# GpSimd shares the low parts of the weights beside the choice of keys, with two pauses and a root moved

## The chip, the cores and the metric

The kernel runs on one core of a Trainium2 chip. The metric is the device time of one execution in microseconds (us). The engines are named as in the profile: PE (matrix products), PEld (its weight loads), DVE (VectorE), ACT (ScalarE), POOL (GpSimd) and SP (SyncE).

## The reference

All in float32, for 512 tokens of width 1024: two hybrid layers (dilated attention, mLSTM, MLP), then one layer with three mixers, which is the one that the change touches:

```python
def _layer(h, ...):
    xn = _rmsnorm(h, norm1_w)
    proj = xn @ w_in
    z, xbc, dt_raw, q, k, v, qi, ki, wi, u, gates = _split_proj(proj)
    xbc = jax.nn.silu(_causal_dwconv(xbc, conv_w, conv_b))
    xs, Bm, Cm = jnp.split(xbc, ...)
    dt = jax.nn.softplus(dt_raw + dt_bias)
    y = _ssd_scan(xh, dt, -jnp.exp(a_log), Bm, Cm)
    y = y + d_skip * xh
    y_ssd = _rmsnorm(y * jax.nn.silu(z), ssd_norm_w)
    y_att = _dsa_attention(qh, kh, vh, qi, ki, wi)
    y_pool = _pool_mixer(u, pool_w, pool_scale)
    g = jax.nn.sigmoid(gates)
    merged = g0 * (y_ssd @ w_up_ssd) + g1 * (y_att @ w_up_attn) + g2 * (y_pool @ w_up_pool)
    h = h + merged @ w_out
    hn = _rmsnorm(h, norm2_w)
    a_part, b_part = jnp.split(hn @ w_ffn_in, 2, axis=-1)
    return h + (jax.nn.silu(a_part) * b_part) @ w_ffn_out

def _dsa_attention(q, k, v, qi, ki, wi):      # for each block of 128 queries
    s = einsum(qi, ki)                        # 4 index heads
    score = einsum(relu(s), wi)               # masked to earlier keys
    idx = top_k(score, 128)                   # the choice of keys
    ...                                       # softmax attention over the chosen keys
```

## The kernel before

**Products.** Each float32 product is three: with a weight split into a high part `wh` and a low part `wl`, and an input into `h` and `l`, `lin` (L281 to L283) adds h·wh, l·wh and h·wl in one PSUM bank `pb`. Weights come as chunks of 128x1024, two tiles of columns each, in the order of their use. `chunk` (L217 to L253) makes one: a DMA on SP's queue brings `wr`, ACT copies it to `wh` (L248), and DVE subtracts the two for `wl` (L249). `wr`, `wh` and `wl` have three buffers each. Where a call has a lead of 2, the two chunks of a pair are worked side by side: here called the first (A) and the second (B) chunk.

**Background work.** The smaller parts are Python generators that `start` registers with a rate. After each group of three products `tick` adds the rate to a counter and takes one step of the generator for each whole number reached; a bare `yield` ends a step, `pause(k)` yields PAUSE[k] times, and `join` runs out what is left. So rates and yields set where the small instructions stand among the large products on each engine, and each engine runs its own instructions in that order. All their PSUM tiles (`br`, `tp`, `bt`, `bb`, `bp`, `yo`, `is`, `bc`, `cs`) share two banks.

**The stage in question.** Behind the convolution the program starts `ssd` in the background of the projections z, qi, k, v and q. The SSD first makes decays: `br` (L1384) is copied to `bs` by ACT, what is left of it is `slo` on DVE (L1389), written into `bs` (L1390). Then, for each of two groups, four transposes to `tp` (L1399), copied as `bt`; sixteen more transposes `tp` (L1408), each four of which DVE scales to `xd` (L1410); states; and a tail of decays: DVE's `le` (L1465), ACT's exponential, POOL's `le` (L1467), PE's `bp` (L1473), `yo` (L1478) and `yd` (L1485), then `cvo` on DVE (L1493), POOL (L1494) and DVE (L1495). After `join(ssd)` the SSD's sum of squares goes through `colsum` (four transposes `cs`, L349, and a reduction, L351), `rsqrt` (twelve small DVE instructions, L365 to L371) and `rowbc` (`hc`, `lc`, two products `dg` on DVE, L339, and two matmuls `bc`, L340). The same root for the layer's input (`rabc`) stands just ahead of `join(ssd)`; it serves eight scalings of `x` on DVE (L1191).

Then `idx`, the indexer, is started beside the gates and the SSD's projection (`branch`), later beside u and the pool mixer. It splits `ki`, makes the scores `is` of each block of queries (L437, L438), rectifies them on ACT (`ir`, L1341), adds them on DVE (L1342), and chooses the keys by 16 rounds of MAX8 and MATCH_REPLACE8 on DVE (L1347, L1348), for three blocks of 256, 384 and 512 keys.

Of the kernel before, what the change touches and what calls it, by code (L numbers as in the profile page):

```python
# [10 lines left out]
F32 = mybir.dt.float32  # L11
# [3 lines left out]
ALU = mybir.AluOpType  # L15
# [4 lines left out]
D = 1024  # L20
NB = 4
# [20 lines left out]
def cols(a, n=P):  # L42
    return np.arange(a, a + n)
# [84 lines left out]

RATE = {"att1": 0.437, "rec": 0.556, "ssd": 0.5, "idx": 0.45, "att2": 0.704, "pool": 0.219}

AHEAD = 2

PAUSE = {"cs": 2, "lf": 5, "cols": 2, "fr": 10, "sum": 1}

LEAD = {"conv": 0, "mo": 0, "ga": 0, "gb": 2, "pa": 2, "pb": 0, "z": 0, "qi": 2, "kv": 2, "q": 2, "br": 2, "up": 2, "u": 2}

# [12 lines left out]
class Build:  # L151
    def __init__(self, nc, tc, ctx, dram, at, recipes):
        self.nc, self.tc = nc, tc
        self.dram, self.at = dram, at
        self.recipes = recipes
        self.nchunk = 0
        pool = lambda **k: ctx.enter_context(tc.tile_pool(**k))
        self.cp = pool(name="cp", bufs=1)
        self.tp = pool(name="tp", bufs=59)
        self.sp = pool(name="sp", bufs=3)  # L160
        self.wp = pool(name="wp", bufs=3)
        self.pm = pool(name="pm", bufs=4, space=PSUM)
        self.pw = pool(name="pw", bufs=2, space=PSUM)
        self.uid = 0
        self.bg = []


    def name(self, s):
# [44 lines left out]
    def pause(self, k):  # L213
        for _ in range(PAUSE[k]):
            yield


    def chunk(self, key, l, rows, cs, keep=False):

        nc = self.nc  # L220
        kt, m = len(rows) // P, len(cs)
        i = self.nchunk
        self.nchunk += 1
        self.recipes.append((key, l, rows, cs))
        n = kt * m
        if i < 2:
            raw = self.raw[i]
        else:
            raw = self.wp.tile([P, CHUNK], F32, name=self.name("wr"), tag="wr")
            nc.sync.dma_start(raw[:, :n], self.dram["w"][i, :, :n])  # L230
        src = raw[:, :n]
        if keep:
            out = [], []
            for k in range(0, kt, 4):
                c = src[:, k * m : min(k + 4, kt) * m]
                for o, part in zip(out, self.split(c, n=c.shape[-1])):
                    o.extend(part[:, x * m : x * m + m] for x in range(min(4, kt - k)))
            return out
        h = self.wp.tile([P, CHUNK], F32R, name=self.name("wh"), tag="wh")
        lo = self.wp.tile([P, CHUNK], F32R, name=self.name("wl"), tag="wl")  # L240
        if i < 2:
            for a, b in FIRST:
                with self.behind(a // P - 1):
                    nc.scalar.activation(h[:, a:b], src[:, a:b], AF.Copy)
                    nc.vector.tensor_tensor(lo[:, a:b], src[:, a:b], h[:, a:b].bitcast(F32), ALU.subtract)
            return tuple(x[:, :n].rearrange("p (k m) -> p k m", k=kt) for x in (h, lo))
        with self.behind(KD - 1 if i == 2 else -1):
            nc.scalar.activation(h[:, :n], src, AF.Copy)  # L248
            nc.vector.tensor_tensor(lo[:, :n], src, h[:, :n].bitcast(F32), ALU.subtract)  # L249
        v = lambda x: x[:, :n].rearrange("p (k m) -> p k m", k=kt)  # L250
        return v(h), v(lo)

# [371 lines left out]
    def hybrid(self, l, xs, acc):  # L624
# [44 lines left out]
        def tok(col, brow, out):  # L669
            bb = self.t("bb")  # L670
            nc.gpsimd.dma_start(bb, self.dram[brow][l : l + 1, :].partition_broadcast(P))

            def ev(b, ps):
                o = self.t("tok")
                v.scalar_tensor_tensor(o, ps, rcol[:, b : b + 1], bb, ALU.mult, ALU.add)
                out.append(o)

            self.lin_tok("w_in", l, cols(col, T), xs, ev)

        def prep(i, x):  # L680
# [352 lines left out]
    def second(self, xs, st):  # L1033
        nc = self.nc
# [5 lines left out]
        rbc, first = None, {}  # L1040
# [11 lines left out]
        def store(dst):  # L1052
            def ev(j, ps):
                o = self.t("p")
                v.tensor_tensor(o, ps, rbc, ALU.mult)
                dst[j] = o

            return ev
# [34 lines left out]
        stz = {"acc": None}  # L1093
        ssd = self.start(self.ssd(xc, dtw3, zs, ys, stz), RATE["ssd"])

# [8 lines left out]
        self.lin_cols("w_in_2", 0, [cols(Z2 + j * P) for j in range(8)], xs, ev_z, lead=LEAD["z"])  # L1104
        qi = [None] * 2
        self.lin_cols("w_in_2", 0, [cols(QI2 + j * P) for j in range(2)], xs, store(qi), lead=LEAD["qi"])
        kv = [None] * 2
        self.lin_cols("w_in_2", 0, [cols(K2), cols(V2)], xs, store(kv), lead=LEAD["kv"])
        vtok = self.t("vtok")
# [9 lines left out]
            q[j] = o  # L1119

        self.lin_cols("w_in_2", 0, [Q2 + QPERM[j * P : j * P + P] for j in range(4)], xs, ev_q, lead=LEAD["q"])
        rabc = self.rowbc(self.rsqrt(first["sum"], NB, 1.0 / D, "rn"))
        self.join(ssd)
        ssum = self.colsum([stz["acc"]])
        sr = self.rsqrt(ssum, NB, 1.0 / D, "rs")
        srb = self.rowbc(sr)
        bias = [None] * NB
        idx = self.start(self.indexer(qi, ki, wi, bias), RATE["idx"])


        m = [None] * 8
# [32 lines left out]
        pool = [None]  # L1164

        def pooled(j):
            if j == 4:
                u = [None] * 4
                self.lin_cols("w_in_2", 0, [cols(U2 + i * P) for i in range(4)], xs, store(u), lead=LEAD["u"])
                pool[0] = self.start(self.pool(u, yp), RATE["pool"])  # L1170

        branch(0, 0, "w_up_ssd_2", ys, extra=srb, hook=pooled)
        self.join(pool[0])

        self.join(idx)
        ya = []
        kk = [self.stack_k(kv[0], x) for x in range(2)]
        att = self.start(
# [6 lines left out]
            ),  # L1185
            RATE["att2"],
        )
# [72 lines left out]
        for tk, c in zip(parts, acc):  # L1260
            n = tk.stop - tk.start
            for j in range(TAIL, 8):
                sq = add(j, tk)
            cs = self.ps("cs")[:, :n]
# [54 lines left out]
    def indexer(self, qi, ki, wi, bias):  # L1319
        nc = self.nc  # L1320
        v = nc.vector
        bias[0] = self.t("b0")
        v.tensor_scalar(bias[0][:, 0:P], self.c("maskI"), NEG, None, ALU.max)
        qA = []
        for h in range(4):
            qA.append(self.stack_q(qi[h // 2], h % 2))
            yield
        B, C = self.split(ki)
        yield
        for I in range(1, NB):  # L1330
            n = P * (I + 1)
            sc = self.t("sc")
            for h in range(4):
                sp = self.ps("is")
                self.dots(sp, qA[h], B, C, I * P, n)
                wcol = wi[:, 4 * I + h : 4 * I + h + 1]
                if h == 0:
                    v.tensor_scalar(sc[:, :n], sp[:, :n], 0.0, wcol, ALU.max, ALU.mult)
                else:
                    r = self.t("ir")  # L1340
                    nc.scalar.activation(r[:, :n], sp[:, :n], AF.Relu)  # L1341
                    v.scalar_tensor_tensor(sc[:, :n], r[:, :n], wcol, sc[:, :n], ALU.mult, ALU.add)  # L1342
                yield
            v.tensor_tensor(sc[:, I * P : n], sc[:, I * P : n], self.c("maskI"), ALU.add)
            for _r in range(16):
                m8 = self.s("m8", 8)
                v.max(m8, sc[:, :n])  # L1347
                v.match_replace(sc[:, :n], m8, sc[:, :n], TAKEN)  # L1348
                yield
            v.tensor_scalar(sc[:, :n], sc[:, :n], TAKEN, NEG, ALU.not_equal, ALU.mult)  # L1350
            bias[I] = sc

    def ssd(self, xc, dtw3, zs, ys, stz):
        nc = self.nc
# [15 lines left out]
        cs = self.ps("cs")  # L1370
        nc.tensor.matmul(cs[:, 0:64], tri, a, start=True, stop=True)
        nc.tensor.matmul(cs[:, 64:128], self.ones, a, start=True, stop=True)
        bt = self.s("sbt", 128, bufs=1)
# [14 lines left out]
        lo = self.t("slo")[:16]  # L1388
        v.tensor_tensor(lo, br[0:16, :], bs[0:16, :].bitcast(F32), ALU.subtract)  # L1389
        v.tensor_copy(bs[32:48, :], lo)  # L1390
        yield
        for gi in range(2):
            sel = self.t("selp", F32R)
            src = self.c("sel")[:, 8 * gi : 8 * gi + 8].unsqueeze(2).to_broadcast([P, 8, 64])
# [4 lines left out]
                nc.tensor.transpose(tp[:, c * P : c * P + P], xc[8 + gi][:, c * P : c * P + P], idn)  # L1399
            btok = self.t("bt")  # L1400
            nc.scalar.copy(btok, tp)
            yield
            xd = [None] * NB
            prev = [None] * NB
            for c in range(NB):
# [188 lines left out]
```

## Time and profile before

| | us |
|---|---|
| median of 3 runs | 2461.04 (2460.28 to 2463.59) |
| the profiled execution, its time | 2463.07 |
| its span | 2461.3 |
| PE busy in it | 2432.2 (99%) |
| DVE, ACT, POOL busy | 1450.0 (59%), 1021.0 (41%), 357.2 (15%) |
| mean granted clock of PE | 0.997 of full speed |

The span runs from the first to the last instruction; the execution's time is 1.8 us longer. A busy PE is not PE at its peak: consecutive products overlap, so a product's length is longer than the distance of two starts, and what counts is the idle time in front of an instruction, with the instruction that ended it. In the timelines, a row is the start, the length, engine, line, operation, output and inputs, shape, count, and in brackets the idle time before it and its releaser.

### The profile page before, as it was taken

What the parts mean: (1) busy time and instruction counts of PE and PEld (TensorE: products, weight loads), DVE (VectorE), ACT (ScalarE), POOL (GpSimd) and SP (SyncE); (2) the same over time, 40 slices, a digit from 0 to 9 for tenths busy, and PEclk for the clock granted to TensorE, in tenths of its full rate; (3) what the DMA queues carried; (4) which work ended last, traced back from release to release, by engine and by line L of the source; (5) the groups of instructions that cost most, each with busy time, mean ns of one, the idle gap of its engine ahead of it and who ended that gap; (6) DMA issues with size and microseconds to landing.
All of it is one profiled execution on the core that took longest, in us unless ns stands there. A gap on an engine that the chain in (4) does not pass through costs nothing.

```text
span 2461.3 us, 28093 instructions
## 1 busy us (share of the span) xinstructions
PE 2432.2 (99%) x10858; PEld 1935.1 (79%) x10858; DVE 1450.0 (59%) x2445; ACT 1021.0 (41%) x1514; POOL 357.2 (15%) x301
## 2 busy tenths in 40 slices
PE   9999999999999999999999999999999999999998
PEld 7877788888887877778888888777777788888887
DVE  6686655433446687655433446867898755434345
ACT  4577534332234387633332324444325533322223
POOL 3410010000311520001000030143222100101010
PEclk9999999999999999999999999999999999999999
DMA  4221223333333322223233233221222222333332
GB/s 160 90 82 52 78 80 97 99 94 94 94 94 94 95 78 69 61 86 101 88 96 95 86 106 95 84 82 52 81 87 70 76 80 92 103 95 92 96 91 72
DMA packets 62821, 216.46 MB, mean 88 GB/s; under 512 B 7136, under 2 KB 10464, under 8 KB 62688
## 3 DMA queue, kind: packets, MB, share of 16 engines
q1 hardware_dynamic: 59840, 210.57, 28.0%
q0 software_dynamic: 800, 2.62, 0.3%
q8 instruction: 85, 1.39, 0.2%
q10 hardware_dynamic: 2048, 1.48, 0.2%
q14 instruction: 48, 0.39, 0.0%
HBM read 212.55 MB, written 2.10 MB: 87 GB/s over the span
## 4 chain that ended last, share of the span: by engine, by line
PE 86%; DVE 8%; ACT 2%; issue 2%; DMA 1%; POOL 0%; SPq 0%; DVEq 0%; ACTq 0%; POOLq 0%
PE pb L281 25%; PE pb L282 25%; PE pb L283 25%; DVE wl L249 2%; PE yp L484 1%; PE pb L320 1%; PE pb L321 1%; PE pb L322 1%; PE PT L465 1%; DVE sc L1348 1%; DVE cv L528 1%; DVE m L1347 1%; PE S L964 1%; PE num L971 1%; DVE A L420 1%
## 5 line engine op out<-in xcount | busy, mean ns | idle before, releaser
L281 PE MATMUL pb<-h,wh 128*128 128x512 f32 x2976 | 1197.5, 402 | 2.8 <-DVE qk L646 2.3
L283 PE MATMUL pb<-h,wl 128*128 128x512 f32 x2976 | 1179.7, 397 | 2.9 <-DVE wl L249 2.9
L282 PE MATMUL pb<-l,wh 128*128 128x512 f32 x2976 | 1179.3, 396 | 0.1
L248 ACT ACTIVATE wh<-wr 128x1024 fp32r<-128x1024 f32 (+1 forms) x393 | 410.8, 1055 | 957.3 <-PE pb L282 681.4
L249 DVE TENSOR_TENSOR wl<-wr,wh 128x1024 fp32r<-128x1024 f32 (+1 forms) x393 | 507.0, 1294 | 285.9 <-ACT wh L248 283.0
L281 PEld LDWEIGHTS pb<-h,wh 128*128 128x128 f32 x2976 | 561.0, 189 | 137.2 <-issue 5.1
L283 PEld LDWEIGHTS pb<-h,wl 128*128 128x128 f32 x2976 | 560.6, 188 | 136.3 <-DVE wl L249 4.8
L282 PEld LDWEIGHTS pb<-l,wh 128*128 128x128 f32 x2976 | 561.3, 189 | 132.8 <-issue 5.2
L823 POOL TENSOR_TENSOR y<-y,rbc 128x512 f32<-128x512 f32 x16 | 24.6, 1540 | 573.0 <-DVE y L821 573.0
L1209 DVE TENSOR_TENSOR f<-pb,rbc 128x512 f32<-128x512 f32 x44 | 30.4, 692 | 124.9 <-PE pb L283 124.9
L266 ACT ACTIVATE h<-f 128x512 fp32r<-128x512 f32 x86 | 54.4, 633 | 109.3 <-DVE f L809 88.2
L1213 POOL TENSOR_TENSOR f<-f,fs 128x512 f32<-128x512 f32 x22 | 38.3, 1740 | 406.6 <-ACT fs L1212 406.6
L831 DVE TENSOR_TENSOR x<-x,pb 128x512 f32<-128x512 f32 x40 | 27.5, 688 | 100.4 <-PE pb L283 100.3
L267 DVE TENSOR_TENSOR l<-f,h 128x512 fp32r<-128x512 f32 x86 | 59.4, 691 | 44.4 <-ACT h L266 44.4
L821 DVE TENSOR_TENSOR y<-y,pb 128x512 f32<-128x512 f32 x32 | 22.0, 689 | 92.5 <-PE pb L283 92.5
L528 DVE SCALAR_TENSOR_TENSOR cv<-cz,par,cv 128x512 f32<-128x512 f32 x84 | 67.6, 805 | 12.4 <-ACT cv L526 11.5
L454 ACT ACTIVATE s<-s,ng 128x128 f32<-128x128 f32 (+3 forms) x96 | 53.5, 558 | 33.8 <-DVE ng L453 33.5
L320 PE MATMUL pb<-wh,h 128*128 128x512 f32 x128 | 51.0, 400 | 0.4 <-DVE gt L724 0.4
L737 DVE TENSOR_TENSOR gate<-pb,rbc 128x512 f32<-128x512 f32 x40 | 27.3, 687 | 40.0 <-PE pb L283 39.9
L321 PE MATMUL pb<-wh,l 128*128 128x512 f32 x128 | 50.8, 397 | 0.0
L322 PE MATMUL pb<-wl,h 128*128 128x512 f32 x128 | 50.5, 396 | 0.0
L788 POOL TENSOR_TENSOR m<-m,m 128x512 f32<-128x512 f32 x16 | 26.0, 1623 | 155.0 <-DVE m L787 155.0
(391 smaller groups left out, 2298.6 us busy)
## 6 DMA issues: line engine op xcount, KB each, us to landing
wr<-in_w_dram SPq DMA_DIRECT2D x381, 512.0 KB, 3.6
wr<-in_w_dram SPq DMA_DIRECT2D x16, 448.0 KB, 3.4
x<-in_x_dram POOLq DMA_DIRECT2D x6, 256.0 KB, 5.8
out_dram<-o SPq DMA_DIRECT2D x4, 256.0 KB, 2.4
out_dram<-o ACTq DMA_DIRECT2D x4, 256.0 KB, 2.7
x<-in_x_dram SPq DMA_DIRECT2D x2, 256.0 KB, 4.3
wr<-in_w_dram SPq DMA_DIRECT2D x4, 128.0 KB, 5.7
wr<-in_w_dram SPq DMA_DIRECT2D x2, 256.0 KB, 7.7
```

The costliest lines, as they stand in the source:

```text
L248: nc.scalar.activation(h[:, :n], src, AF.Copy)
L249: nc.vector.tensor_tensor(lo[:, :n], src, h[:, :n].bitcast(F32), ALU.subtract)
L266: nc.scalar.activation(h[:, :n], src, AF.Copy)
L267: nc.vector.tensor_tensor(lo[:, :n], src, h[:, :n].bitcast(F32), ALU.subtract)
L281: mm(ps[:m, :], a, xh, start=k == 0, stop=False)
L282: mm(ps[:m, :], a, xl, start=False, stop=False)
L283: mm(ps[:m, :], b, xh, start=False, stop=k == n - 1)
L320: mm(ps[b], ah, wh[:, kk, :], start=k == 0, stop=False)
L321: mm(ps[b], al, wh[:, kk, :], start=False, stop=False)
L322: mm(ps[b], ah, wl[:, kk, :], start=False, stop=k == 7)
L454: nc.scalar.activation(s[:, :n], s[:, :n], AF.Exp, bias=ng, scale=-1.0, accum_out=ls)
L528: nc.vector.scalar_tensor_tensor(a, z[:, 1 + j : 1 + j + T], w[:, j : j + 1], a, ALU.mult, ALU.add)
```

## The change

Four edits, all in the third layer:

- While the indexer runs (`shared`, from its start to its join) every chunk with an odd number has its subtraction on GpSimd.
- The SSD pauses two steps where it yielded once: behind `bs`, and behind `bt`. The indexer pauses three steps where it yielded once, behind the split of `ki`.
- The root `rabc` is made behind the projection qi, two projections earlier.
- The rates of `ssd` and `idx` are 0.51 and 0.46, from 0.5 and 0.45.

```diff
-RATE = {..., "ssd": 0.5, "idx": 0.45, ...}
+RATE = {..., "ssd": 0.51, "idx": 0.46, ...}
-PAUSE = {"cs": 2, "lf": 5, "cols": 2, "fr": 10, "sum": 1}
+PAUSE = {"cs": 2, "lf": 5, "cols": 2, "fr": 10, "sum": 1, "bt": 2, "is": 3}
...
+        self.shared = False
...
             nc.scalar.activation(h[:, :n], src, AF.Copy)
-            nc.vector.tensor_tensor(lo[:, :n], src, h[:, :n].bitcast(F32), ALU.subtract)
+            sub = nc.gpsimd if self.shared and i % 2 else nc.vector
+            sub.tensor_tensor(lo[:, :n], src, h[:, :n].bitcast(F32), ALU.subtract)
...
         self.lin_cols("w_in_2", 0, [cols(QI2 + j * P) for j in range(2)], xs, store(qi), lead=LEAD["qi"])
+        rabc = self.rowbc(self.rsqrt(first["sum"], NB, 1.0 / D, "rn"))
...
         self.lin_cols("w_in_2", 0, [Q2 + QPERM[j * P : j * P + P] for j in range(4)], xs, ev_q, lead=LEAD["q"])
-        rabc = self.rowbc(self.rsqrt(first["sum"], NB, 1.0 / D, "rn"))
         self.join(ssd)
...
         idx = self.start(self.indexer(qi, ki, wi, bias), RATE["idx"])
+        self.shared = True
...
         self.join(idx)
+        self.shared = False
...
         B, C = self.split(ki)
-        yield
+        yield from self.pause("is")
...
         v.tensor_copy(bs[32:48, :], lo)
-        yield
+        yield from self.pause("bt")
...
             nc.scalar.copy(btok, tp)
-            yield
+            yield from self.pause("bt")
```

The lines behind these stand three to five lower in the changed kernel (L249 is L252 there, L1408 is L1413, L1467 is L1472). PE's work and SP's queue of weight DMAs are the same; ten subtractions go from DVE to POOL, all of them of first chunks of a pair. Rows below are an engine's instructions in its order, each with line, operation, output and inputs.

**The SSD's first transposes, on PE.** Before, from two products ahead of L1399 to the first L1408:

```order
L283 MATMUL pb_12395<-h_11390,wl_12392 128x512
L1399 MATMUL tp_12404<-first,cvo_11794 128x128 x4
L281 MATMUL pb_12395<-h_11434,wh_12391 128x512
L282 MATMUL pb_12395<-l_11435,wh_12391 128x512
L283 MATMUL pb_12395<-h_11434,wl_12392 128x512
L281 MATMUL pb_12395<-h_11478,wh_12391 128x512
L282 MATMUL pb_12395<-l_11479,wh_12391 128x512
L283 MATMUL pb_12395<-h_11478,wl_12392 128x512
L1408 MATMUL tp_12417<-first,cvo_11880 128x128
```

Of the change, the same transposes (L1404 there) and the products behind them; one more product follows these rows, and then the first L1413:

```order
L286 MATMUL pb_12395<-h_11478,wl_12392 128x512
L1404 MATMUL tp_12410<-first,cvo_11794 128x128 x4
L284 MATMUL pb_12395<-h_11522,wh_12391 128x512
L285 MATMUL pb_12395<-l_11523,wh_12391 128x512
L286 MATMUL pb_12395<-h_11522,wl_12392 128x512
L284 MATMUL pb_12395<-h_11566,wh_12391 128x512
L285 MATMUL pb_12395<-l_11567,wh_12391 128x512
L286 MATMUL pb_12395<-h_11566,wl_12392 128x512
L284 MATMUL pb_12395<-h_11610,wh_12391 128x512
L285 MATMUL pb_12395<-l_11611,wh_12391 128x512
L286 MATMUL pb_12395<-h_11610,wl_12392 128x512
L284 MATMUL pb_12395<-h_11654,wh_12391 128x512
```

Twelve products stand between the transposes and the next ones, where six stood; and the first transposes themselves stand six products later.

**The SSD's tail, on POOL.** `le` and `cvo` are the SSD's decays and outputs. Before:

```order
L1467 TENSOR_TENSOR le_13107<-le_13107,cbs_13010 128x512
L1467 TENSOR_TENSOR le_13122<-le_13122,cbs_13010 128x512
L1494 TENSOR_TENSOR cvo_12138<-cvo_12138,eb_13137 128x384
L1467 TENSOR_TENSOR le_13177<-le_13177,cbs_13010 128x512
L1467 TENSOR_TENSOR le_13192<-le_13192,cbs_13010 128x512
L1494 TENSOR_TENSOR cvo_12181<-cvo_12181,eb_13218 128x384
L1467 TENSOR_TENSOR le_13258<-le_13258,cbs_13010 128x512
L1467 TENSOR_TENSOR le_13273<-le_13273,cbs_13010 128x512
L1494 TENSOR_TENSOR cvo_12224<-cvo_12224,eb_13297 128x384
```

Of the change:

```order
L1472 TENSOR_TENSOR le_13162<-le_13162,cbs_13056 128x512
L252 TENSOR_TENSOR wl_13437<-wr_13434,wh_13436 128x1024
L1499 TENSOR_TENSOR cvo_12138<-cvo_12138,eb_13177 128x384
L1472 TENSOR_TENSOR le_13228<-le_13228,cbs_13056 128x512
L1472 TENSOR_TENSOR le_13243<-le_13243,cbs_13056 128x512
L1499 TENSOR_TENSOR cvo_12181<-cvo_12181,eb_13258 128x384
L252 TENSOR_TENSOR wl_13525<-wr_13522,wh_13524 128x1024
L1472 TENSOR_TENSOR le_13307<-le_13307,cbs_13056 128x512
L1472 TENSOR_TENSOR le_13322<-le_13322,cbs_13056 128x512
L1499 TENSOR_TENSOR cvo_12224<-cvo_12224,eb_13337 128x384
L1499 TENSOR_TENSOR cvo_12267<-cvo_12267,eb_13373 128x384
L252 TENSOR_TENSOR wl_13624<-wr_13621,wh_13623 128x1024
```

Three subtractions for weights that are used after the SSD's join stand among its steps, one ahead of the first `cvo`, one ahead of the third pair of `le`, one behind the last `cvo`.

**The root and the indexer's start, on DVE and PE.** On DVE before, from the input's root (dg_13392) into that of the SSD's sum:

```order
L339 TENSOR_TENSOR dg_13392<-first,hc_13387 128x512
L339 TENSOR_TENSOR dg_13395<-first,lc_13388 128x512
L351 TENSOR_REDUCE cs_13404<-cs_13399 128x4
L1191 SCALAR_TENSOR_TENSOR x_99<-x_99,par_9235,rbc_13386 128x512
L365 TENSOR_SCALAR rsx_13406<-cs_13404 128x4
L1191 SCALAR_TENSOR_TENSOR x_100<-x_100,par_9235,rbc_13386 128x512
L366 TENSOR_SCALAR rsa_13408<-rsx_13406 128x4
L1191 SCALAR_TENSOR_TENSOR x_101<-x_101,par_9235,rbc_13386 128x512
L367 TENSOR_SCALAR rsy_13407<-rsa_13408 128x4
L1191 SCALAR_TENSOR_TENSOR x_102<-x_102,par_9235,rbc_13386 128x512
L369 TENSOR_TENSOR rsa_13408<-rsx_13406,rsy_13407 128x4
L249 TENSOR_TENSOR wl_13543<-wr_13540,wh_13542 128x1024
```

Of the change, from the last step of the SSD on:

```order
L385 TENSOR_TENSOR acc_12686<-acc_12686,sq_13396 128x512
L354 TENSOR_REDUCE cs_13404<-cs_13399 128x4
L368 TENSOR_SCALAR rsx_13406<-cs_13404 128x4
L369 TENSOR_SCALAR rsa_13408<-rsx_13406 128x4
L370 TENSOR_SCALAR rsy_13407<-rsa_13408 128x4
L372 TENSOR_TENSOR rsa_13408<-rsx_13406,rsy_13407 128x4
L373 SCALAR_TENSOR_TENSOR rsa_13408<-rsa_13408,rsy_13407 128x4
L252 TENSOR_TENSOR wl_13532<-wr_13529,wh_13531 128x1024
L374 SCALAR_TENSOR_TENSOR rsy_13407<-rsa_13408,rsy_13407 128x4
L372 TENSOR_TENSOR rsa_13408<-rsx_13406,rsy_13407 128x4
```

The scalings of `x` and the first `dg` are gone from the chain (they stand behind rows of the SSD, some 50 rows earlier), and one subtraction of weights stands in it where two stood. On PE 46 products stood between the transposes `cs` of this sum and its first `bc`, and 22 do now. On PE, the indexer's first products before:

```order
L283 MATMUL pb_13539<-h_13362,wl_13536 128x512
L281 MATMUL pb_13546<-h_13362,wh_13542 128x512
L282 MATMUL pb_13546<-l_13363,wh_13542 128x512
L283 MATMUL pb_13546<-h_13362,wl_13543 128x512
L437 MATMUL is_13509<-h_13498,A_13462 128x256
L437 MATMUL is_13519<-h_13498,A_13471 128x256
L438 MATMUL is_13509<-l_13499,A_13462 128x256
L438 MATMUL is_13519<-l_13499,A_13471 128x256
L437 MATMUL is_13553<-h_13498,A_13480 128x256
L438 MATMUL is_13553<-l_13499,A_13480 128x256
```

and of the change:

```order
L285 MATMUL pb_13528<-l_13284,wh_13524 128x512
L440 MATMUL is_13543<-h_13498,A_13462 128x256
L440 MATMUL is_13553<-h_13498,A_13471 128x256
L286 MATMUL pb_13528<-h_13283,wl_13525 128x512
L284 MATMUL pb_13535<-h_13283,wh_13531 128x512
L285 MATMUL pb_13535<-l_13284,wh_13531 128x512
L441 MATMUL is_13543<-l_13499,A_13462 128x256
L441 MATMUL is_13553<-l_13499,A_13471 128x256
L286 MATMUL pb_13535<-h_13283,wl_13532 128x512
L284 MATMUL pb_13528<-h_13362,wh_13524 128x512
```

They stood in a row, 12 products behind the second `bc`; now the first two stand 15 products behind it, and groups of products of weights stand between them.

## Rows read from the trace of the kernel before

**Rows 1.** The page, busy time of each engine over the whole span.

```profile
PE 2432.2 (99%) x10858; PEld 1935.1 (79%) x10858; DVE 1450.0 (59%) x2445; ACT 1021.0 (41%) x1514; POOL 357.2 (15%) x301
```

**Rows 2.** Waits of PE over the whole span: total us, times, longest.

```profile
PE pb L283 <- DVE wl L249: 2.9, 3, 1.3
PE tp L1408 <- DVE slo L1389: 1.6, 1, 1.6
PE bc L340 <- DVE dg L339: 1.1, 4, 0.3
PE is L437 <- ACT h L266: 0.8, 1, 0.8
PE is L437 <- ACT ir L1341: 0.7, 1, 0.7
PE is L438 <- DVE l L267: 0.5, 1, 0.5
```

**Rows 3.** Windows: PE, PEld, DVE, ACT, POOL busy us (instructions); PE clock; DMA; GB/s.

```profile
1740.00:1780.00 40.00, 37.68 (x157) 29.20 (x155) 34.17 (x75) 15.79 (x23) 4.74 (x4) 0.96 0.17 53
1780.00:1820.00 40.00, 38.73 (x169) 31.42 (x169) 39.03 (x91) 7.50 (x9) 8.68 (x8) 1.00 0.37 109
1820.00:1860.00 40.00, 38.36 (x160) 29.55 (x159) 39.45 (x72) 11.86 (x16) 17.50 (x18) 1.00 0.23 72
```

**Rows 4.** Timeline of DVE, two operations ahead of the SSD's transposes.

```profile
1624.43 1.22 DVE L249 TENSOR_TENSOR wl<-wr,wh 128x1024 fp32r<-128x1024 f32 x1 [1.84 <-ACT wh L248]
1625.57 0.67 DVE L1389 TENSOR_TENSOR slo<-br,bs 16x512 f32<-16x512 f32 x1
```

**Rows 5.** Timeline of PE around the indexer's first products.

```profile
1759.76 0.40 PE L282 MATMUL pb<-l,wh 128*128 128x512 f32 x1
1759.99 0.40 PE L283 MATMUL pb<-h,wl 128*128 128x512 f32 x1
...
1761.19 0.50 PE L437 MATMUL is<-h,A 128*128 128x256 f32 x2 [0.80 <-ACT h L266]
...
1765.41 0.63 PE L281 MATMUL pb<-h,wh 128*128 128x512 f32 x1
1765.84 0.63 PE L282 MATMUL pb<-l,wh 128*128 128x512 f32 x1
```

**Rows 6.** Timeline of POOL: its operations beside the SSD and the gates.

```profile
1621.21 1.30 POOL L532 TENSOR_TENSOR cvo<-cv,sg 128x512 f32<-128x512 f32 x1 [3.88 <-ACT sg L530]
...
1711.25 1.28 POOL L1467 TENSOR_TENSOR le<-le,cbs 128x512 f32<-128x512 f32 x1 [1.00 <-ACT le L1466]
1714.04 1.02 POOL L1494 TENSOR_TENSOR cvo<-cvo,eb 128x384 f32<-128x384 f32 x1 [1.51 <-DVE cvo L1493]
...
1723.39 1.92 POOL L1494 TENSOR_TENSOR cvo<-cvo,eb 128x384 f32<-128x384 f32 x1 [0.89 <-DVE cvo L1493]
...
1779.12 4.10 POOL L1141 TENSOR_TENSOR gate<-gate,rbc 128x512 f32<-128x512 f32 x2 [10.28 <-ACT gate L1139]
```

**Rows 7.** Timeline of DVE: operations with two inputs beside those of POOL.

```profile
1621.30 1.29 DVE L1379 TENSOR_TENSOR sdec<-sbt 128x64 f32<-128x64 f32 x1
...
1709.51 1.82 DVE L249 TENSOR_TENSOR wl<-wr,wh 128x1024 fp32r<-128x1024 f32 x1
...
1780.09 1.98 DVE L249 TENSOR_TENSOR wl<-wr,wh 128x1024 fp32r<-128x1024 f32 x1
```

**Rows 8.** Timeline of DVE: the root of the SSD's sum.

```profile
1745.74 0.69 DVE L351 TENSOR_REDUCE cs<-cs 128x4 f32<-128x512 f32 x1 [0.72 <-PE cs L349]
1746.35 0.74 DVE L1191 SCALAR_TENSOR_TENSOR x<-x,par,rbc 128x512 f32<-128x512 f32 x1
1747.01 0.16 DVE L365 TENSOR_SCALAR rsx<-cs 128x4 f32<-128x4 f32 x1
...
1749.28 1.22 DVE L249 TENSOR_TENSOR wl<-wr,wh 128x1024 fp32r<-128x1024 f32 x1
...
1756.04 0.69 DVE L339 TENSOR_TENSOR dg<-first,lc 128x512 fp32r<-128x512 f32 x1
```

More of the change, by code (lines that the diff above doesn't have):

```diff
@@ L127, in params2 @@
     return pack(parts)
-RATE = {"att1": 0.437, "rec": 0.556, "ssd": 0.5, "idx": 0.45, "att2": 0.704, "pool": 0.219}
+RATE = {"att1": 0.437, "rec": 0.556, "ssd": 0.51, "idx": 0.46, "att2": 0.704, "pool": 0.219}
 AHEAD = 2
-PAUSE = {"cs": 2, "lf": 5, "cols": 2, "fr": 10, "sum": 1}
+PAUSE = {"cs": 2, "lf": 5, "cols": 2, "fr": 10, "sum": 1, "bt": 2, "is": 3}
 LEAD = {"conv": 0, "mo": 0, "ga": 0, "gb": 2, "pa": 2, "pb": 0, "z": 0, "qi": 2, "kv": 2, "q": 2, "br": 2, "up": 2, "u": 2}
```

## Prediction

> **What bounds the kernel now.** The page comes first: PE is busy 99% of the span [rows 1], so a change can only win what PE waits or what its clock loses. The list of PE's waits is next [rows 2]. There the reader sees that the waits which the four edits can reach are short: 2.9 us in three waits of weight products for DVE's `wl`, 1.6 us in one of the SSD's transposes `tp` for `slo`, 1.1 us in four waits of `bc`, of which the root that moves has 0.3, and 0.8, 0.7 and 0.5 us of the indexer's products `is`. Then the windows over the choice of keys [rows 3]: DVE is busy 39.03 and 39.45 of 40 us there, more than PE, while POOL works 8.68 and 17.50. In the window ahead of them PE has its one lower granted clock, 0.96.
>
> The timelines give the causes. `slo` is behind a subtraction of weights on DVE [rows 4], and the transposes need the PSUM bank that it frees. The first `is` waits 0.80 us for ACT's split of `ki` and, behind that, two more times; then two starts of weight products are 0.43 us apart, where they were 0.23 us before the waits [rows 5]. That is PE at 1.2 GHz in place of 2.4, after a stretch with gaps. A mean of 0.96 over 40 us is 4% of 40, so 1.6 us were lost by it.
>
> The sum is made against the profiled execution, 2463.07 us. The median of the runs, 2461.04, stands 2.0 lower, and I take 2.0 off at the end. What a measurement can tell from no change is about 0.2%, 4.9 us: faster means under 2456.1, slower over 2466.0.
>
> **What it should win.**
> - *The SSD's transposes.* Six more products stand ahead of `tp` (L1399) and twelve in place of six behind it, so the waiting transposes stand 12 x 0.23 = 2.8 us later against `slo`, which does not move. That is over the wait of 1.6 [rows 2, 4]: gain 1.6, late next nothing that I see (`xd` is made from the same transposes, and the SSD's rate is 2% higher).
> - *The root moved forward.* Its two `dg`, two `bc` and twelve small DVE instructions go among the SSD's second group, where PE has weight products to do; 0.3 us of wait [rows 2] goes. The eight scalings of `x` at 0.74 us [rows 8] go there too, off the chain of the next root; DVE has room there.
> - *The indexer's products.* They start 15 products behind the second `bc`, not 12, which is 0.7 us against the 0.8 waited for `h`; and products of weights now stand between them, so the waits for `l` and `ir` find cover. Of 0.8 + 0.7 + 0.5 = 2.0 us I leave 0.4. If the gaps go, so does the low clock, 1.6 us [rows 2, 3]. Gain 3.2, between 1.0 (waits half left, clock too) and 3.6.
> - *The subtractions on POOL.* Ten at 1.22 us [rows 4] are 12.2 us less on a DVE that is full. The waits for `wl` are of second chunks of a pair, which stay on DVE, so they come forward with DVE. The ten are all first chunks, whose buffers come free a chunk earlier (48 products, 11 us), so POOL has time. I leave 0.5 of 2.9: gain 2.4, between 0 and 2.9.
>
> Sum of gains: 1.6 + 0.3 + 3.2 + 2.4 = 7.5.
>
> **What it should cost.** No row shows a subtraction of 128x1024 on POOL. The nearest are 1.28 us for 128x512 and 1.02 for 128x384 [rows 6]: 0.26 for 128 columns, so 1.28 + 4 x 0.26 = 2.3; twice 1.28 is 2.6. I take 2.4. The upper end is the 128x384 that took 1.92 [rows 6], 1.9 times as long: 4.5.
> - *The SSD's tail.* One subtraction stands ahead of the first `cvo` of POOL, one ahead of a pair of `le`. Behind the late `cvo` DVE waits with the next `le` queued behind it, and PE with `bp` and `yd` behind that. Each can cost PE between 0 (POOL and PE had the slack) and 2.4. From the lengths of the rows I work out some 1.7 for the first and 1.3 for the second, since POOL was idle 1.5 us ahead of its `cvo` and 1.0 ahead of `le` [rows 6]: 3.0, between 0 and 4.8.
> - *The SSD's root.* From the reduction to the end of the second `dg` the chain took 1745.74 to 1756.73 [rows 8], 11.0 us, with 46 products of cover (10.6 us). Now 22 stand there: 5.1 us. The chain loses the eight scalings (8 x 0.66 start to start) and one subtraction (1.2): 11.0 - 5.3 - 1.2 = 4.5 us are left, and the first `bc` needs only the first `dg`, 0.7 sooner. With the 0.7 us that DVE idled for `cs` it is 4.5 against 5.1, no wait at all, if nothing stands in between. But a POOL subtraction stands right there too, behind the last `cvo`, and that holds DVE up.
>
> What shows that is a pair of rows: `sdec`, 128x64, took 1.29 us on DVE beginning 0.09 us behind a POOL operation of 1.30 us, and both end together [rows 6, 7]. A subtraction took 1.98 beside POOL's 4.10 us of gates, and 1.82 beside `le`, not 1.22 [rows 4, 6, 7]. So a DVE operation with two inputs in SBUF can stand still until POOL's ends: the root's chain can lose up to 2.4 us by it. I take 1.3, between 0 and 3.2, and for the others, that a subtraction on DVE now and then takes the rest of a POOL one, which is in the 0.5 that I left above.
>
> The Trainium skill, "SBUF — State Buffer", section "Who interferes with whom", speaks against this change: a DVE instruction with two SBUF inputs contends with a GpSimd one that reads SBUF, and whoever issues first has the shared ports for the whole instruction. The trace agrees (1.29 for a 128x64 operation). Taken strictly, it would make each of the ten a lock of its full length, which is the last rival below.
>
> The two rates and the order of SP's queue cost nothing: the DMAs and PE's work are the same, a yield more or less only moves rows. A chunk's buffer comes free about 1.2 us later on POOL, covered by the 11 us of the chunk that is being used.
>
> Sum: -7.5 + 3.0 + 1.3 = -3.2; 2463.07 - 3.2 - 2.0 = 2457.9, so **2458 us**.
>
> **The rivals.**
> - *No new wait.* The SSD's tail has slack and the root's chain misses POOL's operation. For it: POOL idles 35 of 40 us in the window of the root [rows 3], and 3.88 us ahead of a step of the SSD [rows 6]. Against it: PE's SSD steps follow closely upon each other. -7.5, or -8.4 with nothing left of the waits: 2453.6 to 2452.7.
> - *All is given back.* The tail costs 4.8 and the root 3.2, at their upper ends: +0.5, 2461.5; with the `wl` waits unchanged, 2463.9. For it: the same two rows that show DVE stopped. If the root's `bc` waits that long, the clock may fall as it did at `is`.
> - *The pauses don't do it.* The order moves as said, but the split of `ki` is later too and `is` and `tp` wait as before: gains 0.3 + 2.4 against 4.3, 2462.6. Little speaks for it; it would be a DVE full of what moved.
> - *Slower: DVE is locked by POOL beside the choice of keys.* Each subtraction moved saves DVE 1.2 us. If it stops DVE for more than 1.2 on the mean, DVE has more to do than before, and there it has 0.5 to 1 us left in 40 [rows 3], so PE pays. At the upper length, 4.5, and an arrival in the middle, it stops 2.25, net 1.05 for seven subtractions: +7.4, with 4.3 of other costs and 5.1 of gains: +6.6, 2467.6. For it: the 4.10 us of two gates that should take 2.6 [rows 6]. Against it: POOL already worked 8.68 us beside a full DVE in the window of 1780 to 1820, and PE was busy 38.73 of 40 all the same [rows 3].
>
> **How the numbers follow.** The sum as forecast 0.42, with its own range 2455 to 2461; no new wait 0.27; all given back 0.17; the pauses in vain 0.04; slower 0.10. A third of the forecast, 0.14, lies under 2456.1. Faster: 0.27 + 0.14 = 0.41. Same: 0.28 + 0.17 + 0.04 = 0.49. Slower: 0.10. The range, 2452 to 2464, reaches over the first two rivals and leaves out the slow case and a little at the low end.
>
> **What would show it.** Right: no wait of `tp` for `slo`; PE's clock 1.00 in the window of the indexer's start; under 1 us waited for `wl`; POOL's subtraction near 2.4 us; new waits of `bp` or `yd` near 1.7 and 1.3 us in the SSD's tail, and of `bc` for `dg` near 1.3. Wrong in the good direction: none of the new waits. Wrong in the bad one: a clock under 1.00 behind `bc`, POOL's subtraction over 4 us, and `wl` on DVE at over 2.4 us beside the choice of keys, with waits for `wl` over 3 us.

## The result and the profile after

The changed kernel takes 2477.55 us (median of 6 runs, 2476.49 to 2478.83) against 2460.93 for the kernel before: a ratio of 1.0067 with a 95% interval of 1.0057 to 1.0077, so 16.6 us slower. 2458 was forecast, with a range up to 2464. The profiled execution took 2477.80, its span is 2476.0.

The page of the changed kernel, engines' busy time:

```profile
PE 2436.7 (98%) x10858; PEld 1940.2 (78%) x10858; DVE 1456.2 (59%) x2435; ACT 1020.7 (41%) x1514; POOL 378.6 (15%) x311
```

DVE has ten instructions fewer than before [rows 1] and is busy 6.2 us longer, not 12.2 shorter (5.4 of this comes without the sharing, as experiment 1 shows). PE's list of waits, total, times and longest:

```profile
PE pb L286 <- DVE wl L252: 8.1, 5, 4.3
PE bc L343 <- DVE dg L342: 3.4, 5, 2.2
PE is L440 <- DVE sc L1343: 2.6, 1, 2.6
PE bp L1478 <- DVE le L1470: 2.3, 3, 1.8
```

The waits of `tp` and most of those of `is` for `h`, `l` and `ir` [rows 2] are gone, as forecast. In their place stand 8.1 us for `wl` in place of 2.9, 3.4 for `bc` in place of 1.1, 2.6 of `is` for the bank that `sc` holds on DVE, and 2.3 of `bp`. No wait of PE is for a `wl` that POOL made. The windows, with the columns of [rows 3]:

```profile
1740.00:1780.00 40.00, 35.14 (x159) 26.70 (x158) 30.84 (x60) 13.67 (x21) 11.18 (x8) 0.96 0.21 67
1780.00:1820.00 40.00, 39.85 (x174) 31.98 (x172) 35.57 (x80) 10.56 (x13) 15.77 (x12) 1.00 0.24 79
1820.00:1860.00 40.00, 32.57 (x119) 24.48 (x120) 35.55 (x66) 8.11 (x11) 15.71 (x13) 0.88 0.27 86
```

The window in the middle is better than before (39.85 busy, was 38.73). The last one has only 32.57 of 40 and a granted clock of 0.88; before it had 38.36 and 1.00 [rows 3]. 12% of 40 us is 4.8 us. Some 0.9 of it lies in PE's longest wait itself (from 1850.81 to 1855.51 the granted clock is 0.81), so the clock alone cost some 3.9 us there.

Set beside each other by the position in the sequence of weight products, the two traces are level at 1600 us. The changed kernel is 2.6 us ahead behind the SSD's first transposes, 4.5 behind at the end of the SSD, 6.4 behind at 1780, 5.4 at 1820, 9.3 at 1830 and 15.1 at 1850; from 1900 on the distance stays at 16.1. (Where pauses put a step of the background later, a trace counts as ahead until the step is done.)

Why DVE saved nothing is in its timeline (start, length, operation, idle before):

```profile
1717.71 2.17 DVE L252 TENSOR_TENSOR wl<-wr,wh 128x1024 fp32r<-128x1024 f32 x1
...
1753.90 2.36 DVE L374 SCALAR_TENSOR_TENSOR rsy<-rsa,rsy 128x4 f32<-128x4 f32 x1
...
1770.64 2.30 DVE L1347 SCALAR_TENSOR_TENSOR sc<-ir,wi,sc 128x256 f32<-128x256 f32 x1
...
1773.66 1.21 DVE L252 TENSOR_TENSOR wl<-wr,wh 128x1024 fp32r<-128x1024 f32 x1
...
1820.86 1.84 DVE L1314 TENSOR_TENSOR pt<-pt,p 128x16 f32<-128x16 f32 x1
...
1839.98 2.30 DVE L1347 SCALAR_TENSOR_TENSOR sc<-ir,wi,sc 128x512 f32<-128x512 f32 x1
...
1844.52 1.75 DVE L1312 SCALAR_TENSOR_TENSOR pt<-pt,p 128x496 f32<-128x496 f32 x1 [1.20 <-POOL pt L1306]
...
1850.61 0.68 DVE L1353 MATCH_REPLACE8 sc<-m,sc 128x512 f32<-128x512 f32 x1
...
1854.24 1.22 DVE L252 TENSOR_TENSOR wl<-wr,wh 128x1024 fp32r<-128x1024 f32 x1
```

The row of 1753.90 is an operation on 128x4. One of that size took 0.16 us [rows 8]; this one took 2.36. `sc` (L1347) of 128x256 takes 0.48 undisturbed (so in the kernel before, at 1764.25) and took 2.30 at 1770.64. POOL at those times:

```profile
1718.77 3.38 POOL L252 TENSOR_TENSOR wl<-wr,wh 128x1024 fp32r<-128x1024 f32 x1
...
1753.66 2.57 POOL L252 TENSOR_TENSOR wl<-wr,wh 128x1024 fp32r<-128x1024 f32 x1 [6.18 <-ACT wh L249]
...
1770.26 2.40 POOL L252 TENSOR_TENSOR wl<-wr,wh 128x1024 fp32r<-128x1024 f32 x1 [0.42 <-ACT wh L249]
...
1820.00 2.68 POOL L252 TENSOR_TENSOR wl<-wr,wh 128x1024 fp32r<-128x1024 f32 x1 [3.51 <-ACT wh L249]
...
1839.15 2.58 POOL L252 TENSOR_TENSOR wl<-wr,wh 128x1024 fp32r<-128x1024 f32 x1 [2.30 <-ACT wh L249]
1841.69 1.49 POOL L1306 TENSOR_TENSOR pt<-pt 128x510 f32<-128x510 f32 x1
...
1850.43 2.37 POOL L252 TENSOR_TENSOR wl<-wr,wh 128x1024 fp32r<-128x1024 f32 x1 [2.86 <-ACT wh L249]
```

The long DVE rows of 1753.90, 1770.64, 1820.86 and 1839.98 have two inputs in SBUF. Each begins while a POOL subtraction runs, and ends with it or up to 0.6 us behind it: 1753.90 + 2.36 = 1756.26, POOL 1753.66 + 2.57 = 1756.23; 1770.64 + 2.30 = 1772.94, POOL to 1772.66.

Not every subtraction does this. In the whole trace six of the ten stop one such operation, for some 1.5 to 2.2 us, 10.5 in sum. Two, of 3.38 and 3.50 us, met a subtraction of DVE's and were held up themselves. The other two met only operations that kept their length: the SSD's `le`, which has an input in PSUM, and rounds of the choice of keys (0.68 us for the row of 1850.61, beside POOL's 1850.43, as for its like elsewhere).

The POOL rows of 1839.15 and 1841.69 show a second thing. The pool mixer's `pt` stands behind the subtraction, which itself had to wait for ACT's copy. DVE idles 1.20 us for `pt` and is stopped once more (row 1844.52), here by a product of POOL's gates (1844.44, 1.29 us) and not by a subtraction; the weights' `wl` of 1854.24 is behind that. PE at these places:

```profile
1728.38 0.47 PE L1478 MATMUL bp<-bs,selp 128*128 128x512 f32 x1 [1.80 <-DVE le L1470]
...
1758.58 0.47 PE L343 MATMUL bc<-dg,onesr 128*128 128x512 f32 x1 [2.19 <-DVE dg L342]
...
1774.93 0.61 PE L286 MATMUL pb<-h,wl 128*128 128x512 f32 x1 [2.32 <-DVE wl L252]
...
1832.91 0.56 PE L440 MATMUL is<-h,A 128*128 128x512 f32 x1 [2.65 <-DVE sc L1343]
...
1855.51 0.79 PE L286 MATMUL pb<-h,wl 128*128 128x512 f32 x1 [4.31 <-DVE wl L252]
1856.11 0.63 PE L284 MATMUL pb<-h,wh 128*128 128x512 f32 x1
1856.53 0.63 PE L285 MATMUL pb<-l,wh 128*128 128x512 f32 x1
```

`bp` waits 1.80 us. `bc` waits 2.19, with the stop of 1753.90 in its chain; the weights wait 2.32 for the `wl` of 1773.66, behind the stop of 1770.64; `is` waits 2.65, with the stop of 1820.86 ahead of it in DVE's order. The wait for `wl` of 4.31 us is followed by products whose starts lie 0.42 apart, the level of 1.2 GHz.

### The profile page after: what moved, and what is told of

Its sections match the earlier page's. It is cut to its first block, busy times and chain, and to the rows that moved or that the text cites. A ratio compares the mean times of both kernels' runs of the same rounds, so it can differ in the third digit from the quotient of the medians.

```text
span 2476.0 us, 28108 instructions
## 1 busy us (share of the span) xinstructions
PE 2436.7 (98%) x10858; PEld 1940.2 (78%) x10858; DVE 1456.2 (59%) x2435; ACT 1020.7 (41%) x1514; POOL 378.6 (15%) x311
## 3 DMA queue, kind: packets, MB, share of 16 engines
q10 hardware_dynamic: 2048, 1.48, 0.2%
## 5 line engine op out<-in xcount | busy, mean ns | idle before, releaser
L249 ACT ACTIVATE wh<-wr 128x1024 fp32r<-128x1024 f32 (+1 forms) x393 | 411.3, 1055 | 959.6 <-PE pb L285 673.8
L286 PEld LDWEIGHTS pb<-h,wl 128*128 128x128 f32 x2976 | 562.5, 189 | 142.3 <-DVE wl L252 12.2
L252 DVE TENSOR_TENSOR wl<-wr,wh 128x1024 fp32r<-128x1024 f32 (+1 forms) x383 | 495.3, 1297 | 293.6 <-ACT wh L249 290.8
```

Source lines behind the costliest of these rows:

```text
L252: sub.tensor_tensor(lo[:, :n], src, h[:, :n].bitcast(F32), ALU.subtract)
L286: mm(ps[:m, :], b, xh, start=False, stop=k == n - 1)
```

## Experiments

Three theories at first. **L**: DVE operations with two inputs stand still until POOL's subtraction ends. **Q**: POOL's own steps, and DVE behind them, queue behind a subtraction. **O**: the pauses, the root and the rates put steps where they wait, whoever subtracts.

**1. The change with every subtraction on DVE** (`-        self.shared = True`).

> The change with every subtraction on DVE again; pauses, root and rates as changed. Theory L (a DVE operation with two SBUF inputs stands still until POOL's subtraction ends) and theory Q (POOL's own steps queue behind its subtractions) both: the loss goes, 2453 to 2462 us. Theory O (the pauses, the root and the rates put steps where they wait, whoever subtracts): it stays over 2470.

Measured: 2464.92 us, ratio 1.0014 (1.0005 to 1.0023). The sharing is most of the loss, but the rest of the change, for which 5 us of gain were forecast, is 3.4 slower than before. Waits of PE, and two windows:

```profile
PE pb L286 <- DVE wl L252: 5.5, 5, 1.6
PE yd L1489 <- POOL le L1471: 1.7, 3, 1.1
PE bp L1477 <- DVE le L1469: 1.6, 3, 0.8
PE is L440 <- ACT h L269: 0.3, 1, 0.3
```

```profile
1700.00:1740.00 40.00, 37.82 (x197) 27.54 (x195) 35.37 (x66) 13.04 (x20) 14.46 (x10) 1.00 0.21 66
1740.00:1780.00 40.00, 38.66 (x179) 29.88 (x179) 30.22 (x64) 17.16 (x25) 6.53 (x7) 1.00 0.22 67
```

`is` waits 0.3 and the clock is 1.00 in the window where it was 0.96: that part came as forecast. `yd` is new and `bp` longer (0.3 before), in the SSD's second half: 37.82 of 40 us busy, where the kernel before had 39.71:

```profile
1700.00:1740.00 40.00, 39.71 (x223) 30.91 (x222) 32.15 (x64) 15.97 (x24) 15.69 (x12) 1.00 0.26 80
```

`wl` waits 5.5, where it was 2.9. DVE is busy 1455.4 us here: its work grew by 5.4 us without any sharing.

**2. The sharing alone**, in the kernel before (the `sub` line and the flag, nothing else).

> The kernel before with the sharing alone; its pauses, root and rates as before. L and Q: 2468 to 2478 us. O: 2458 to 2462.

Measured: 2474.21 us, 1.0054 (1.004 to 1.0067). L or Q. The two parts add up: 2477.55 - 2464.92 = 12.6 us for the sharing within the change, some 13 alone.

**3. The first three shared subtractions on DVE again** (`if self.shared and i % 2 and i >= self.share_from`).

> The change with the first three shared subtractions (the two in the SSD's tail and the one in the root's chain) on DVE, seven on POOL. L and Q: the wait of bp (2.0 us), of bc (2.4) and of the wl that follows (2.5) with 1.6 of clock go, the later ones (2.8, 4.5 and their clock) stay: 2468 to 2472 us. O: as the change, 2475 to 2479.

Measured: 2474.89 us, 1.0051 (1.0038 to 1.0065). A miss: only 2.7 us came back. The waits of `bp` and `bc` shrank to 1.6 and 1.3 in total, but `wl` stayed at 7.9 and the clock fell in the next two windows (0.92 and 0.91). The seven later ones carry most of the loss.

**4. POOL writes but does not read.**

```diff
-            sub = nc.gpsimd if self.shared and i % 2 else nc.vector
-            sub.tensor_tensor(lo[:, :n], src, h[:, :n].bitcast(F32), ALU.subtract)
+            if self.shared and i % 2:
+                nc.gpsimd.memset(lo[:, :n].bitcast(F32), 0.0)
+                nc.gpsimd.memset(lo[:, :n].bitcast(F32), 0.0)
+            else:
+                nc.vector.tensor_tensor(lo[:, :n], src, h[:, :n].bitcast(F32), ALU.subtract)
```

This kernel leaves the low parts of ten chunks out of its sums.

> The change with two fills of the ten tiles on POOL in place of each subtraction (the low parts of those ten chunks are zero, left out of the sums): POOL is busy about as long but reads no SBUF. L: DVE's operations of two inputs keep their lengths and the time is 2453 to 2462 us. Q: POOL's steps and DVE behind them wait as in the change, over 2470.

Measured: 2459.73 us, 0.9992 (0.9983 to 1.0001). As L forecast. The page:

```profile
PE 2430.2 (99%) x10858; PEld 1932.4 (79%) x10858; DVE 1444.1 (59%) x2435; ACT 1020.4 (42%) x1514; POOL 371.6 (15%) x321
```

DVE is busy 12.1 us less than in the change, with as many instructions: about all of the 12.2 us that the ten subtractions took off DVE had come back as stops, 1.2 us for each subtraction on the mean. But these fills, 0.95 us each, do not wait for ACT's copy and are done ahead of POOL's other steps, so Q is not excluded.

**5. The subtraction in four pieces** (`for a in range(0, n, 256)` around it).

> The change with each subtraction on POOL in four pieces of 256 columns; POOL is busy at least as long (about 3.0 us in place of 2.4). Theory L (the whole length of one POOL instruction is what stops DVE): a stop is at most some 0.8 us, most of the loss goes, 2460 to 2468 us. Theory Q (POOL's own queue): as slow as the change or slower, over 2475.

Measured: 2471.86 us, 1.0051 (1.0037 to 1.0065). Between the theories: 5.7 us came back of the 17.8 between the change and experiment 4.

```profile
PE 2433.5 (99%) x10858; PEld 1934.1 (78%) x10858; DVE 1446.9 (59%) x2435; ACT 1020.1 (41%) x1514; POOL 385.5 (16%) x341
```

DVE is nearly as free as in experiment 4 (1446.9 against 1444.1), so its stops are shorter now in sum; yet PE waits. DVE, POOL and PE around the longest wait:

```profile
1839.35 1.75 DVE L1315 SCALAR_TENSOR_TENSOR pt<-pt,p 128x496 f32<-128x496 f32 x1 [3.57 <-POOL pt L1309]
...
1849.08 1.22 DVE L255 TENSOR_TENSOR wl<-wr,wh 128x1024 fp32r<-128x1024 f32 x1
```

```profile
1833.41 2.17 POOL L253 TENSOR_TENSOR wl<-wr,wh 128x256 fp32r<-128x256 f32 x2 [1.52 <-ACT wh L249]
1837.04 1.04 POOL L1309 TENSOR_TENSOR pt<-pt 128x510 f32<-128x510 f32 x1
```

```profile
1850.35 0.80 PE L289 MATMUL pb<-h,wl 128*128 128x512 f32 x1 [4.89 <-DVE wl L255]
```

DVE idles 3.57 us for the pool mixer's `pt`, which stands on POOL behind a subtraction of 3.67 us, which had stood idle for ACT's copy. Five rounds of the choice of keys and then the next `wl` (1849.08) are queued on DVE behind that `pt`, and PE waits 4.89 us for the `wl`. That wait is Q. But one stop is not shortened by the cutting, that of the root's chain:

```profile
1753.38 0.69 DVE L377 SCALAR_TENSOR_TENSOR rsy<-rsa,rsy 128x4 f32<-128x4 f32 x1
1754.11 0.66 DVE L375 TENSOR_TENSOR rsa<-rsx,rsy 128x4 f32<-128x4 f32 x1
1754.80 0.66 DVE L376 SCALAR_TENSOR_TENSOR rsa<-rsa,rsy 128x4 f32<-128x4 f32 x1
1755.50 0.65 DVE L377 SCALAR_TENSOR_TENSOR rsy<-rsa,rsy 128x4 f32<-128x4 f32 x1
```

Four operations that took 0.16 us [rows 8] are stopped by one piece each, 2.0 us in sum where the one stop was 2.2, and `bc` still waits 2.0. So a part of what the pieces leave over is L.

**6. The queue without the reading.** Three fills, two of them on the raw tile, so that they must wait for ACT's copy.

```diff
...
+            if self.shared and i % 2:
+                nc.gpsimd.memset(lo[:, :n].bitcast(F32), 0.0)
+                nc.gpsimd.memset(src, 0.0)
+                nc.gpsimd.memset(src, 0.0)
...
```

This kernel, too, leaves out the low parts of ten chunks.

> The change with fills in place of the ten subtractions: one of the low tile, then two of the raw tile, which have to wait for ACT's copy as the subtraction did (the low parts of those chunks are zero, left out of the sums). POOL is held as long and waits for the same, but reads no SBUF, so DVE is never stopped by it. If the stops (L) are all of the loss: 2458 to 2462 us. If the queue behind the waiting POOL instruction (Q) is all of it: 2474 to 2479. Both: 2464 to 2472.

Measured: 2464.85 us, 1.002 (1.0011 to 1.0029), so both. From these medians the sharing comes apart: DVE's relief 2464.92 - 2459.73 = 5.2 us won; POOL's queue 2464.85 - 2459.73 = 5.1 lost; the stops 2477.55 - 2464.85 = 12.7 lost. The lengths of fills and subtraction are near each other, not equal (0.95 and twice 0.95 behind the copy, 2.40), and POOL's steps do not stand in quite the same order, so the shares are estimates. The positions of PE's products in the traces, from 1600 to 1950, give 4.8, 6.5 and 10.5 for the same three, so they are good to some two us. The positions also say where the loss lies, in the change's own times: of the stops' share, 5.7 us between 1720 and 1780 (`bc`, then `wl`) and 3.3 between 1820 and 1834 (`is`); of the queue's, 4.3 between 1850 and 1860, at the wait behind the pool mixer.

**7. In pieces, and only the four ahead of the pool mixer** (`self.shared = False` before u's projection).

> The change with the subtractions on POOL in pieces of 256 columns, and only the four of them ahead of the pool mixer: the six that share POOL's queue with the pool mixer's steps are on DVE again. In the version with all ten in pieces the weights' wait of 4.9 us follows 3.6 us in which DVE idles for the pool mixer's step on POOL. If that queue is what the pieces leave over (Q): 2463 to 2467 us. If it is DVE's stops by the pieces or the rest of the change: 2469 to 2473.

Measured: 2466.46 us, 1.0022 (1.0014 to 1.0031). 5.4 us better than with all ten in pieces, though six subtractions, 7.3 us, are back on DVE (that takes away the pieces' stops there too, not the queue alone); the wait of 4.9 is gone and the longest for `wl` is 1.6. The 1.5 us that are left over experiment 1 lie at the SSD's tail and root, where POOL still subtracts: `bp` waits 2.8 in all and `bc` 3.2.

The rest of the change: **R** says that the root's eight scalings of `x` burden the SSD's second half, **P** that the pauses push its tail against the join.

**8. Experiment 1 with the root where it was.**

> The two pauses and the two rates, the root where it was, every subtraction on DVE. Theory R (the root's eight scalings of x load DVE in the SSD's second half, so that bp, yd and h come late there): 2457 to 2461 us. Theory P (a pause or rate presses the SSD's tail against its join, whoever scales x): 2463 to 2467, as with the root.

Measured: 2467.17 us, 1.003 (1.002 to 1.0041). R falls: without the move it is slower still.

**9. The root alone**, in the kernel before.

> The kernel before with the root moved and nothing else. R: slower than before by 2 to 5 us, 2463 to 2466. P: the wait of bc (0.3 us) goes, 2460 to 2462.

Measured: 2459.91 us, 0.9997 (0.9989 to 1.0006). P. By the positions of the weight products, 2.7 us are lost in the SSD's second half up to 1740 and 4.2 won by 1770, where `is` no longer waits; at the end the trace is 0.5 us ahead in the stage.

**10. The indexer's pause alone** (`"is": 3`).

> The kernel before with the pause of the indexer alone. If the waits of is (2.0 us) and the clock lost behind them (1.6) are both gone by this pause: 2457 to 2459. If only the waits go: about 2460. If the later rounds of the choice of keys slip against their weights instead: 2461 to 2464.

Measured: 2462.43 us, 1.0011 (1.0002 to 1.002): the third case. PE's waits:

```profile
PE pb L283 <- DVE wl L249: 3.8, 2, 2.5
PE is L437 <- ACT h L266: 0.8, 1, 0.8
```

In this order the first four products of `is` stand where they stood, 13 products behind the second `bc`; the pause moved only what comes behind them. So the wait for `h` is 0.8 as before, and `wl` waits 3.8 in place of 2.9.

**11. The SSD's pauses alone** (`"bt": 2`).

> The kernel before with the two pauses of the SSD alone, its rate as it was. If the wait of the transposes (1.6 us) goes and nothing comes for it: 2459 to 2460. P: the SSD's tail, two to four steps later, meets its join: 2462 to 2465.

Measured: 2463.54 us, 1.0012 (1.0003 to 1.0021). P. The wait of `tp` is gone, and PE's timeline shows what came:

```profile
1746.71 0.63 PE L349 MATMUL cs<-first,acc 128*128 128x128 f32 x4 [0.96 <-DVE acc L382]
...
1760.07 0.51 PE L437 MATMUL is<-h,A 128*128 128x256 f32 x2 [1.48 <-ACT h L266]
```

The sum's transposes wait 0.96 us for `acc` and the indexer 1.48 for `h`, not 0.80 [rows 5]: in this order 34 products lie between `cs` and the first `bc`, 46 before. (This is one of the shorter executions, 2460.59 us. By the positions it still loses 1.8 us in the stage.)

**12. The same pauses, and the SSD's rate at 0.53** for 0.5.

> The kernel before with the two pauses of the SSD and its rate at 0.53 in place of 0.5, which puts the SSD's last products back where they stood. Theory P (the pauses' three steps push the tail against the join): the wait of the transposes (1.6 us) goes and nothing comes for it, 2458 to 2460 us. If the pauses cost in another way: as with the pauses alone, 2462 to 2465.

Measured: 2460.47 us, 1.0003 (0.9994 to 1.0012). The tail stands at the very places of before, and the 3 us are back; the 1.6 of `tp` is not seen on top: by the positions the trace is 2.6 us ahead behind the transposes and has given it back by 1720.

**13. As 12, the input's root behind the indexer's join.**

> The kernel before with the SSD's pauses at the rate of 0.53 and the root of the input behind the indexer's join, so that its eight scalings of x leave the chain of the SSD's root and the SSD's tail both, every subtraction on DVE. If the scalings in that chain are what makes is wait (2.0 us and 1.6 of clock): 2455 to 2458. If the chain's wait only moves to bc or wl: 2459 to 2462.

Measured: 2460.09 us, 1.0 (0.9991 to 1.0009). That is the range of the second case, but not for its reason: `bc` waits 1.2 us and `wl` 2.1, no more than before. The windows of the indexer's start and of the attention's:

```profile
1740.00:1780.00 40.00, 38.01 (x166) 29.44 (x165) 36.66 (x85) 14.60 (x21) 6.25 (x4) 1.00 0.23 74
1860.00:1900.00 40.00, 37.18 (x170) 27.38 (x169) 34.31 (x82) 22.37 (x45) 4.29 (x4) 0.96 0.22 66
```

The first is at a clock of 1.00, where it was 0.96; a gain of some 4 us that stood at 1830 is lost at the attention's start, with the scalings now among its steps (37.18 of 40, clock 0.96).

**14. As 12, the root just ahead of the scalings, behind the attention's join.**

```diff
-        rabc = self.rowbc(self.rsqrt(first["sum"], NB, 1.0 / D, "rn"))
         self.join(ssd)
...
         self.join(att)
+        rabc = self.rowbc(self.rsqrt(first["sum"], NB, 1.0 / D, "rn"))
         for k in range(KD):
```

> The SSD's pauses at the rate of 0.53 with the input's root just ahead of the scalings of x, behind the join of the attention, where DVE is busy 10 to 12 of 20 us; every subtraction on DVE. If the eight scalings cost wherever DVE is full and nothing where it has room: 2454 to 2458 us, as the version with the root behind the indexer's join won 4 to 5 us before its own start of the attention and lost them there. If the root's chain stops PE at the join instead: 2459 to 2462.

Measured: 2456.4 us, 0.9986 (0.9977 to 0.9995), better than both kernels.

```profile
1740.00:1780.00 40.00, 38.00 (x166) 29.66 (x166) 36.60 (x87) 14.17 (x20) 6.26 (x4) 1.00 0.26 79
1820.00:1860.00 40.00, 39.27 (x163) 30.18 (x163) 39.65 (x74) 11.97 (x15) 16.81 (x18) 1.00 0.25 79
1860.00:1900.00 40.00, 38.96 (x192) 30.10 (x191) 32.37 (x81) 27.25 (x53) 8.11 (x4) 1.00 0.24 70
```

All three windows are at a clock of 1.00, `is` waits for nothing, `wl` waits 2.1 us.

## Why the prediction was wrong, point by point

- *The SSD's transposes, gain 1.6*: the wait went, as forecast. That the step costs nothing else was wrong: "late next nothing that I see" overlooked that three more steps move the SSD's tail and `acc` back against its join. Alone the two pauses lose 2.9 us (experiment 11), and the rate of 0.51 does not make up for three steps; 0.53 does (12).
- *The indexer's products, gain 3.2*: right in the place (no wait for `l` or `ir`, 0.3 for `h`, the clock at 1.00 in experiment 1), but the pause alone does not do it (10). The pause never moved the first of these products; it is the scalings of `x` leaving the chain that bring `h` in time (9, 14); with the pauses and without the move (8) `h` is waited for 3.2 us. The count was off by one, too: before, the first `is` stood 13 products behind the second `bc` in the trace, not 12, so 15 is worth 0.5 us and not 0.7.
- *The moved root, 0.3 and "DVE has room there"*: wrong. What it wins at the indexer it loses in the SSD's second half (9); it is worth something where DVE really has room (14).
- *The subtractions on POOL, gain 2.4*: **this is the step that failed.** Its length, estimated at 2.4, measured 2.37 to 2.85 us but for the two that were held up. But the stops, for which the forecast kept "the 0.5 that I left", took back 12.1 us of 12.2 (4), and they fall on the chains that PE waits for: in place of 2.4 won, the sharing lost 12.6. The last rival named the mechanism; I gave it 0.10, because POOL had been busy beside a full DVE already, without asking which operations DVE ran then. Its sum was not right either. It let PE pay for what DVE has to do over all, and at the 1.2 us for each subtraction that came, that is nothing. What PE pays is that a few stops of 1.5 to 2.2 us stand in its chains, while the relief falls elsewhere (6). The clock was lacking, too: two further stretches at 1.2 GHz, some 3.9 us in one window.
- *The order on POOL* was read for the SSD's tail and not for the pool mixer. That queue is worth about 5 us (6), most of it in one wait, and 7 fits.
- *The costs that were forecast*: `bp` 1.7, measured 1.80, which is luck as a price of the sharing: experiment 1, with nothing shared, waits 1.6 for `bp` and 1.7 for `yd`, and up to 1750 the change loses no more than it does. `bc` 1.3, measured 2.19, is within its bounds and has the cause that was named; the wait of the third pair of `le` did not come (0.7 us in all for `yd`).

The Trainium skill, "SBUF — State Buffer", section "Who interferes with whom", says that DVE with two SBUF inputs contends with a GpSimd instruction that reads SBUF, not with one that only writes it. The traces agree with both halves: 2.36 us for a 128x4 operation beside the subtraction, and 12.1 us less on DVE when POOL only fills.

That POOL's queue and DVE's stops are the sharing's loss is shown by experiments 1, 4 and 6, and 5 and 7 fit; how the 17.8 us divide between them is an estimate from fills of nearly the same length. Why experiment 12 does not keep the 1.6 us of `tp`, why DVE's work grew by 5.4 us in experiment 1, and why the root back in its place (8) is worse than moved (1), was not tried further.

## What to carry to other kernels

Count what work moved to GpSimd does to the DVE operations that run beside it: here one with two SBUF inputs, however small, waited for the end of a GpSimd subtraction that ran already, and the rounds of the choice of keys did not. So a subtraction that costs 1.2 us on DVE and 2.4 on GpSimd may free nothing, and cutting it in pieces does not help a chain of small operations beside it. Read the whole of GpSimd's new order for steps behind which DVE waits, and ask whether the moved instruction itself waits for a third engine. And a pause or a moved chain takes its cover from what stands behind it: place work where the engine that carries it has room in the windows, and change rate and pauses together.

## What the runs showed of the hardware that was not expected

A stop works in both directions: POOL's first subtraction took 3.38 us, not 2.40, with DVE's own subtraction (1717.71, 2.17 us) already under way when it began, and with POOL's work in pieces a subtraction lasted up to 4.09 us where the shortest took 2.79. And PE's clock added to the price of the waits: the granted clock of the windows between 1740 and 1900 is 6.8 us short of full speed (0.96, 0.88 and 0.99 of 40 us each) where the kernel before lost 1.6. Without the 0.9 that lies in a wait itself, that is some 4 of the 16 us.
